# Weight sums of the third product, and the residual's sums of squares, on VectorE instead of GpSimd

## The chip, the cores and the metric

The kernel runs on one core of a Trainium2 chip. The time is device microseconds of one execution, given as the median of several runs.

## The reference

A two-layer decoder trunk over 512 tokens of width 1024. Layer 0 joins native sparse attention with memory cross-attention, layer 1 joins dilated sliding-window attention with memory cross-attention. Each layer ends in the part that the change touches:

```python
def rmsnorm(x, g):
    x32 = x.astype(jnp.float32)
    y = x32 * lax.rsqrt(jnp.mean(x32 * x32, axis=-1, keepdims=True) + EPS)
    return (y * g.astype(jnp.float32)).astype(x.dtype)

def squared_relu_mlp(h, w_up, w_down):
    return jnp.square(jax.nn.relu(h @ w_up)) @ w_down
...
    for layer in range(DEPTH):
        ...
        x = x + squared_relu_mlp(rmsnorm(x, mlp_norm[layer]), w_up[layer], w_down[layer])
```

`w_up` is 1024 x 4096 and `w_down` 4096 x 1024 per layer.

## The kernel before

All of it is float32. A product is made of three matmuls in a packed format (fp32r): each operand is split into a high half, a rounding copy made by ScalarE (line 237 for weights, 282 for activations), and a low half, the rest, made by VectorE (lines 239 and 285). `mm3` multiplies high by high (line 244), then high by low and low by high (line 247).

`mlp` runs a layer's MLP in four quarters of 1024 hidden columns. A quarter has eight steps of the up projection (`n` from 0 to 7, 24 matmuls each: weights through `wload`, Relu and Square on ScalarE at lines 1253 and 1254), and then the down projection as one level of a fast matrix scheme with seven products in place of eight. Each product takes a combination of activation blocks (`combos`, line 1145, makes the combined ones `s12` and `s4`) and a combination of four weight blocks `B[0]` to `B[3]`. The products run in this order, each over two halves `h` of the weights, with 24 matmuls:

| order | code | weights | PSUM | activations |
|---|---|---|---|---|
| P1 | `product(X, blk(0, 0), w11)` | `B[0]` | acc | `s_qk` |
| P2 | `product(Z, blk(0, H), w3)` | `T = B[1] + B[3]` | ps | `s_qk` |
| P3 | `product(Y, s2, w2)` | `T + B[0]` | pt | `s_act` |
| P4 | `product(Z, blk(4, H), w4, True)` | `T + B[0] + B[2]` | ps | `s_qk` |
| P5 | `product(V, s1, w1)` | `U = B[1] + B[0]` | pt | `s_act` |
| P6 | `product(V, s4, w22, True)` | `B[3]` | pt | `s_x` |
| P7 | `product(X, blk(4, 0), ..., True)` | `B[2]` | acc | `s_qk` |

The block sums are running sums in place: `addto` (line 1131) adds a freshly loaded tile to two tiles of 128 x 512, and `wpieces` splits a summed pair into high and low. `w3` splits `T` for P2 and then adds `B[0]` (kept in `b11`) to it, which gives P3's weights; `w2` splits those and then adds `B[2]`, which gives P4's. In each quarter `addto` runs 16 instructions: four that begin `T` during the up projection, four that begin `U`, four in `w3`, four in `w2`. All are on GpSimd. A split weight tile (`s_w`) has four buffers, a loaded one (`s_st`) three, and the activations of a step (`s_p`) six.

The results are scaled per token by `r`, the inverse mean square of the residual, since Relu squared lets the normalisation be applied behind both projections. `inverse` makes `r` in the first quarter of each layer, behind step 0: for each of the eight residual tiles `square` takes the square on ScalarE (line 450) and adds it to one running tile (a copy at line 455, then seven adds at line 457), and four small matmuls (line 482) sum over the partitions. `square` runs the adds on GpSimd unless an engine is given. `r` is first used by `into` (line 1333), behind P2.

The code is written as a plain program; a scheduler in the framework fixes the order of each engine's instructions when the kernel is built, from its own estimate of times, and adds the semaphores. Engines run their own instructions in that order. PE is TensorE, DVE VectorE, ACT ScalarE, POOL GpSimd, SP the queue that issues most loads.

Of the kernel before, what the change touches and what calls it, by code (L numbers as in the profile page):

```python
# [12 lines left out]
ALU = mybir.AluOpType  # L13
# [154 lines left out]
class K:  # L168
# [956 lines left out]
            nc.vector.tensor_tensor(out=self.x[m], in0=ps, in1=xo, op=ALU.add)  # L1125


    def addto(self, out, a, b):

        for i, (o, x) in enumerate(zip(out, a)):  # L1130
            self.nc.gpsimd.tensor_tensor(out=o, in0=x, in1=b[:, i * 512 : (i + 1) * 512], op=ALU.add)  # L1131

    def wpieces(self, t):

# [21 lines left out]
    def mlp(self, l):  # L1156


        nc, ins = self.nc, self.ins
        H = S // 2  # L1160
        x = self.x
# [16 lines left out]
        def inverse():  # L1178

            for k in range(KT):  # L1180
                self.square(k, x[k])
            ps = self.ps(self.pO, [P, NB])
            self.sumsq(ps, self.sq, True, True)
            r, n = [self.c(f"{n}{l}", [P, NB]) for n in ("r2", "n2")]
            nc.vector.tensor_scalar(out=r, in0=ps, scalar1=1.0 / D, scalar2=EPS, op0=ALU.mult, op1=ALU.add)
            nc.vector.reciprocal(out=r, in_=r)
            nc.vector.tensor_scalar(out=n, in0=r, scalar1=-1.0, scalar2=None, op0=ALU.mult)
            return r, n
# [47 lines left out]
        for q in range(4):  # L1236
            a, A12, A4 = [None] * 8, [], []
            B = [ins["w_db"][l, q, i] for i in range(4)]
            U, T = [], []
            for n in range(8):  # L1240
# [25 lines left out]
                if q == 0 and n == 0:  # L1266
                    r, nr = inverse()
# [5 lines left out]
                if n in (5, 6):  # L1273

                    t = [self.t("x", [P, 512]) for _ in range(2)]
# [16 lines left out]
            b11 = []  # L1292
# [11 lines left out]
            def w3(h):  # L1304

                t = T[2 * h : 2 * h + 2]
                w = self.wpieces(t)
                self.addto(t, t, b11[h])
                return w

            def w2(h):
# [31 lines left out]
            for u in range(2):  # L1343
                if q == 0:
                    nc.scalar.activation(G[u], X[u], AF.Copy)
                else:
                    add(G[u], X[u])
            product(Z, blk(0, H), w3)
            into(Z, 1, 1, True)
            Y = two(self.pT)  # L1350
# [463 lines left out]
```

## Time and profile before

| | |
|---|---|
| median of 3 runs | 1276.46 us (1275.83 to 1279.62) |
| profiled execution | 1277.1 us, span 1275.3 us |
| granted TensorE clock, mean | 0.997 |
| TensorE (matmul) busy | 1240.4 us, 97% |
| VectorE busy | 990.8 us, 78% |
| ScalarE busy | 763.3 us, 60% |
| GpSimd busy | 469.4 us, 37% |
| DMA | 139.11 MB, mean 109 GB/s |

Times within the profile are counted from the start of the span. Layer 0's MLP lies between some 325 and 695 us, layer 1's between some 925 us and the end. In a row of the order of time the columns are start, length, engine, line, operation, output<-inputs and shape; in brackets stands the idle time of the engine before it and what ended that. A row of a stretch gives its bounds, its length, then for each engine busy time and number of instructions (PE, weight loads, DVE, ACT, POOL), then the granted clock, the DMA share and GB/s. A row of waits names who waited, for whom, the total in us, the count and the longest.

### The profile page before, as it was taken

To read this page: it belongs to the slowest core of one execution; us is meant where nothing else is said; L and a number is where in the kernel's file an instruction comes from. 1 tells how busy PE (TensorE), PEld (TensorE's weight loads), DVE (VectorE), ACT (ScalarE), POOL (GpSimd) and SP (SyncE) were. 2 spreads that over 40 slices of the span, in tenths; PEclk is the share of its full clock that TensorE was granted. 3 is DMA by queue.
4 is the path that set the end of the run, shared out by engine and by line. 5 is a ranking of instruction groups with operands and counts; after the bars stand their busy time and mean duration, and the time that the engine had idled before them with its cause. 6 is when DMAs were issued, how large, how long until landed. Compare 5 with 4: busy or idle time off the path is not lost.

```text
span 1275.3 us, 18580 instructions
## 1 busy us (share of the span) xinstructions
PE 1240.4 (97%) x6445; PEld 1013.5 (79%) x6445; DVE 990.8 (78%) x1745; ACT 763.3 (60%) x1763; POOL 469.4 (37%) x497
## 2 busy tenths in 40 slices
PE   9998999999999999999999999999999999999998
PEld 8776777677787887888888899888688788888886
DVE  6868878864669678687799968887679868779687
ACT  6666767773466464554656567887776455464462
POOL 0666464533165142260342612222435226034241
PEclk9999999999999999999999999999999999999999
DMA  8312311023432525325235332113241532624423
GB/s 312 112 58 69 100 34 59 10 75 106 151 99 77 175 79 171 125 83 185 97 98 179 104 116 64 62 35 96 69 155 67 178 124 79 187 94 139 141 83 116
DMA packets 52718, 139.11 MB, mean 109 GB/s; under 512 B 5680, under 2 KB 14896, under 8 KB 52624
## 3 DMA queue, kind: packets, MB, share of 16 engines
q1 hardware_dynamic: 51568, 135.50, 33.4%
q0 software_dynamic: 480, 1.38, 0.3%
q8 instruction: 51, 0.84, 0.3%
q10 hardware_dynamic: 576, 1.05, 0.2%
q14 instruction: 43, 0.35, 0.1%
HBM read 132.66 MB, written 5.24 MB: 108 GB/s over the span
## 4 chain that ended last, share of the span: by engine, by line
PE 74%; DVE 17%; ACT 4%; issue 2%; DMA 1%; POOL 1%; SPq 0%; POOLq 0%; DVEq 0%; ACTq 0%
PE s_ps L247 23%; PE s_acc L247 12%; PE s_ps L244 11%; DVE s_w L239 6%; PE s_acc L244 6%; PE s_pt L247 5%; PE s_pt L244 3%; DVE s_p L1145 2%; PE s_po L1080 2%; DVE s_qk L285 1%; PE s_acc L845 1%; ACT s_w L237 1%; PE s_pt L1067 1%; PE s_ps L1031 1%; DVE s_pt L1333 1%
## 5 line engine op out<-in xcount | busy, mean ns | idle before, releaser
L247 PE MATMUL s_ps<-s_act,s_w 128*128 128x512 f32 x1184 | 366.0, 390 | 0.0
L239 DVE TENSOR_TENSOR s_w<-s_st,s_w 128x1024 fp32r<-128x1024 f32 (+4 forms) x161 | 191.1, 1189 | 133.5 <-ACT s_w L237 133.2
L247 PEld LDWEIGHTS s_ps<-s_act,s_w 128*128 128x128 f32 x1184 | 221.8, 188 | 45.7 <-DVE s_act L285 0.4
L237 ACT ACTIVATE s_w<-s_st 128x1024 fp32r<-128x1024 f32 (+4 forms) x182 | 165.7, 918 | 131.0 <-PE s_pt L247 35.6
L244 PE MATMUL s_ps<-s_act,s_w 128*128 128x512 f32 x592 | 231.6, 393 | 3.1 <-DVE s_x L817 1.7
L247 PE MATMUL s_acc<-s_w,s_act 128*128 128x512 f32 (+2 forms) x608 | 169.7, 360 | 2.0 <-DVE s_w L239 1.5
L1131 POOL TENSOR_TENSOR s_x<-s_x,s_st 128x512 f32<-128x512 f32 x64 | 106.0, 1681 | 90.8 <-DVE s_w L239 90.8
L244 PEld LDWEIGHTS s_ps<-s_act,s_w 128*128 128x128 f32 x592 | 110.9, 188 | 28.4 <-ACT s_act L282 3.2
L247 PEld LDWEIGHTS s_acc<-s_w,s_act 128*128 128x128 f32 x608 | 108.9, 190 | 13.1 <-DVE s_w L239 1.6
L244 PE MATMUL s_acc<-s_w,s_act 128*128 128x512 f32 (+2 forms) x304 | 111.0, 370 | 1.9 <-ACT s_w L237 1.9
L1131 POOL TENSOR_TENSOR s_x<-s_qki,s_st 128x512 f32<-128x512 f32 x16 | 26.5, 1654 | 214.9 <-DMA s_st<-in_w_db_dram 195.3
L676 POOL TENSOR_SCALAR s_p<-s_p,s_cr 128x256 f32<-128x256 f32 (+3 forms) x128 | 68.0, 545 | 71.6 <-DVE s_cr L1043 33.4
L239 DVE TENSOR_TENSOR s_w<-s_x,s_w 128x512 fp32r<-128x512 f32 x96 | 88.7, 965 | 5.6 <-ACT s_w L237 5.6
L247 PE MATMUL s_pt<-s_w,s_act 128*128 128x512 f32 x288 | 90.0, 399 | 2.6 <-DVE s_w L239 2.6
L285 DVE TENSOR_TENSOR s_qk<-s_p,s_qk 128x256 fp32r<-128x256 f32 (+1 forms) x96 | 83.9, 886 | 2.8 <-ACT s_qk L282 1.8
L237 ACT ACTIVATE s_w<-s_x 128x512 fp32r<-128x512 f32 x96 | 56.8, 624 | 41.1 <-POOL s_x L1131 41.1
L247 PE MATMUL s_ps<-s_w,s_qk 128*128 128x512 f32 x256 | 78.5, 393 | 2.5 <-DVE s_w L239 2.5
L247 PE MATMUL s_acc<-s_w,s_qk 128*128 128x512 f32 x256 | 76.4, 390 | 0.1
L282 ACT ACTIVATE s_qk<-s_p 128x256 fp32r<-128x256 f32 (+1 forms) x96 | 47.0, 489 | 45.1 <-DVE s_p L1259 42.8
L247 PEld LDWEIGHTS s_pt<-s_w,s_act 128*128 128x128 f32 x288 | 54.0, 191 | 16.9 <-DVE s_w L239 6.0
L1253 ACT ACTIVATE s_p<-s_ps 128x512 f32<-128x512 f32 x64 | 37.8, 591 | 46.8 <-PE s_ps L247 44.4
L244 PEld LDWEIGHTS s_acc<-s_w,s_act 128*128 128x128 f32 x304 | 57.5, 190 | 7.3 <-ACT s_w L237 2.0
(336 smaller groups left out, 2735.8 us busy)
## 6 DMA issues: line engine op xcount, KB each, us to landing
s_st<-in_w_db_dram SPq DMA_DIRECT2D x80, 512.0 KB, 3.6
s_st<-in_w_up_dram SPq DMA_DIRECT2D x64, 512.0 KB, 3.9
s_st<-in_w_bq_dram SPq DMA_DIRECT2D x16, 384.0 KB, 3.1
s_st<-in_w_ag_dram SPq DMA_DIRECT2D x11, 512.0 KB, 4.0
s_act<-in_w_c_dram SPq DMA_DIRECT2D x8, 512.0 KB, 5.8
s_st<-in_w_mem_dram SPq DMA_DIRECT2D x8, 512.0 KB, 3.6
s_st<-in_w_ao_dram SPq DMA_DIRECT2D x16, 256.0 KB, 2.7
s_tq<-in_w_db_dram SPq DMA_DIRECT2D x16, 256.0 KB, 3.2
```

The source lines that it names most:

```text
L237: self.high = nc.scalar.activation(w[:, 0], st, AF.Copy)
L239: self.low = e.tensor_tensor(out=w[:, 1], in0=st, in1=w[:, 0], op=ALU.subtract)
L244: mm(ps, lh[0], rh[0], start=start, stop=False, skip_group_check=again)
L247: self.last = mm(ps, lh[i], rh[j], start=False, stop=stop and i != wr, skip_group_check=again)
L282: nc.scalar.activation(dst[:, 0], src, AF.Copy)
L285: nc.vector.tensor_tensor(out=dst[:, 1], in0=src, in1=dst[:, 0], op=ALU.subtract)
L676: self.nc.gpsimd.tensor_scalar(out=p, in0=p, scalar1=c, scalar2=1.0, op0=ALU.mult, op1=ALU.mult)
L845: nc.tensor.matmul(ps, tbf[:, i].rearrange("p g c -> p (g c)"), ws[j][:, i * 256 : (i + 1) * 256], start=j == 0 and i == 0, stop=j == 3 an ...
L1080: nc.tensor.matmul(O[x * 64 : x * 64 + 64, q0 + o : q0 + 256], v[:, j, br, :], st[x][br][:, j, o:256], start=half == 0 and br == 1 and j = ...
L1131: self.nc.gpsimd.tensor_tensor(out=o, in0=x, in1=b[:, i * 512 : (i + 1) * 512], op=ALU.add)
L1145: tt = lambda o, x, y, op: nc.vector.tensor_tensor(out=o, in0=x, in1=y, op=op)
L1253: nc.scalar.activation(u, ps, AF.Relu)
```

## The change

`addto` takes an engine, and GpSimd stays its default. `w3` gives it VectorE: these four sums of each quarter, 32 in the kernel, move. `inverse` gives `square` VectorE: the copy and the seven adds of each layer, 16 instructions, move. The other twelve sums of a quarter stay on GpSimd.

```diff
-    def addto(self, out, a, b):
+    def addto(self, out, a, b, e=None):
 
         for i, (o, x) in enumerate(zip(out, a)):
-            self.nc.gpsimd.tensor_tensor(out=o, in0=x, in1=b[:, i * 512 : (i + 1) * 512], op=ALU.add)
+            (e or self.nc.gpsimd).tensor_tensor(out=o, in0=x, in1=b[:, i * 512 : (i + 1) * 512], op=ALU.add)
...
         def inverse():
 
             for k in range(KT):
-                self.square(k, x[k])
+                self.square(k, x[k], nc.vector)
...
                 t = T[2 * h : 2 * h + 2]
                 w = self.wpieces(t)
-                self.addto(t, t, b11[h])
+                self.addto(t, t, b11[h], nc.vector)
                 return w
```

For the first residual tile, `square` on VectorE also orders the ScalarE square behind the last weight split issued (lines 451 and 452). The scheduler then arranges the whole order anew. Three places of it follow, as pieces of the difference between the two orders. On VectorE, in quarter 1 of layer 0 from the second split of P2's weights on (`s_w_5338` is P2's second half, `s_w_5361` P3's first, `s_x_...` the tiles of `T`, `s_p_1277` and `s_qk_5262` the last step's activations):

```order
+L1131 TENSOR_TENSOR s_x_5177<-s_x_5177,s_st_5279 128x512
 L239 TENSOR_TENSOR s_w_5338<-s_x_5223,s_w_5338 128x512
+L1131 TENSOR_TENSOR s_x_5178<-s_x_5178,s_st_5279 128x512
 L239 TENSOR_TENSOR s_w_5338<-s_x_5224,s_w_5338 128x512
 L1145 TENSOR_TENSOR s_p_1277_5265<-s_p_1266_5213,s_p_1275_5259 128x256
+L1131 TENSOR_TENSOR s_x_5223<-s_x_5223,s_st_5298 128x512
 L285 TENSOR_TENSOR s_qk_5262<-s_p_1275_5259,s_qk_5262 128x512
+L239 TENSOR_TENSOR s_w_5361<-s_x_5177,s_w_5361 128x512
+L1131 TENSOR_TENSOR s_x_5224<-s_x_5224,s_st_5298 128x512
+L239 TENSOR_TENSOR s_w_5361<-s_x_5178,s_w_5361 128x512
```

The four sums are new here, and the two splits of P3's first half have moved up to them. On VectorE a little later in the same quarter (`s_act_5269` is the low half of the last `s12`, `s_x_5272` of the last `s4`, `s_w_5382` P3's second half, `s_raw` the running result `G`):

```order
-L285 TENSOR_TENSOR s_act_5269<-s_p_1277_5265,s_act_5269 128x512
-L285 TENSOR_TENSOR s_x_5272<-s_p_1268_5219,s_x_5272 128x256
 L1337 TENSOR_TENSOR s_raw_4676<-s_acc_5276,s_raw_4676 128x512
-L239 TENSOR_TENSOR s_w_5361<-s_x_5178,s_w_5361 128x512
 L239 TENSOR_TENSOR s_w_5382<-s_x_5223,s_w_5382 128x512
 L239 TENSOR_TENSOR s_w_5382<-s_x_5224,s_w_5382 128x512
+L1145 TENSOR_TENSOR s_p_1268_5219<-s_p_1275_5259,s_p_1277_5265 128x256
+L285 TENSOR_TENSOR s_act_5269<-s_p_1277_5265,s_act_5269 128x512
```

The low half of the last `s12` has moved from ahead of P3's second half to behind it, and that of `s4` further still. On VectorE at the start of layer 0's MLP (`s_w_4491` and `s_w_4543` are the up projection's weights of steps 5 and 6):

```order
+L455 COPY s_raw_4240<-s_p_1106_4238 128x512
+L457 TENSOR_TENSOR s_raw_4240<-s_raw_4240,s_p_1108_4242 128x512
+L457 TENSOR_TENSOR s_raw_4240<-s_raw_4240,s_p_1109_4245 128x512
 L285 TENSOR_TENSOR s_qk_4231<-s_p_1105_4234,s_qk_4231 128x256
+L457 TENSOR_TENSOR s_raw_4240<-s_raw_4240,s_p_1110_4248 128x512
+L457 TENSOR_TENSOR s_raw_4240<-s_raw_4240,s_p_1111_4251 128x512
 L239 TENSOR_TENSOR s_w_4491<-s_st_4489,s_w_4491 128x1024
-L239 TENSOR_TENSOR s_w_4543<-s_st_4541,s_w_4543 128x1024
```

The squares' copy and adds stand ahead of the split of step 5's weights, and the split of step 6's has moved behind them. The order of the SP queue stays the same but for one weight load of layer 1's attention, which moves ahead of one store.

## The prediction

> **What bounds the kernel now.** I read the page's busy times first, then the stretches by stage, then TensorE's waits, then the order of time around each of them.
>
> ```profile
> PE 1240.4 (97%) x6445; PEld 1013.5 (79%) x6445; DVE 990.8 (78%) x1745; ACT 763.3 (60%) x1763; POOL 469.4 (37%) x497
> 506.00:588.40 82.40, 81.98 (x362) 67.41 (x361) 64.47 (x81) 41.90 (x67) 26.69 (x16) 1.00 0.40 129
> PE s_pt L247 <- DVE s_w L239: 2.6, 4, 1.0
> PE s_ps L247 <- DVE s_w L239: 2.5, 7, 0.4
> ```
>
> TensorE (PE) is busy for 97% of the span, and the third quarter of layer 0's MLP (second row) has 81.98 us of PE in 82.40. So only a wait of PE can be won. In the MLP such waits have nearly one cause: PE stands before the low half of a split weight tile (L239), 5.1 us in 11 places. What they cost is more, because a matmul after a pause starts late; the order of time shows it. I count the seven products of a quarter as they run, P1 to P7, 24 matmuls each: P2 takes w3's weights (the change's "third product"), P3 w2's, P4 w4's. Third quarter, then layer 0's first quarter, then layer 1's:
>
> ```profile
> 567.82 0.39 PE L244 MATMUL s_pt<-s_w,s_act 128*128 128x512 f32 x1
> 573.32 0.39 PE L244 MATMUL s_ps<-s_w,s_qk 128*128 128x512 f32 x1
> 574.81 0.73 PE L247 MATMUL s_ps<-s_w,s_qk 128*128 128x512 f32 x2 [0.42 <-DVE s_w L239]
> 579.50 0.39 PE L244 MATMUL s_pt<-s_w,s_act 128*128 128x512 f32 x1
> 584.94 0.62 PE L244 MATMUL s_acc<-s_w,s_qk 128*128 128x512 f32 x2
> ...
> 400.91 0.39 PE L244 MATMUL s_pt<-s_w,s_act 128*128 128x512 f32 x1
> 404.22 1.20 PE L247 MATMUL s_pt<-s_w,s_act 128*128 128x512 f32 x4 [0.99 <-DVE s_w L239]
> 408.66 0.39 PE L244 MATMUL s_ps<-s_w,s_qk 128*128 128x512 f32 x1
> 414.60 0.39 PE L244 MATMUL s_pt<-s_w,s_act 128*128 128x512 f32 x1
> ...
> 992.06 0.39 PE L244 MATMUL s_pt<-s_w,s_act 128*128 128x512 f32 x1
> 995.41 1.90 PE L247 MATMUL s_pt<-s_w,s_act 128*128 128x512 f32 x4 [0.99 <-DVE s_w L239]
> 1001.45 0.39 PE L244 MATMUL s_ps<-s_w,s_qk 128*128 128x512 f32 x1
> 995.50:999.50 4.00, 4.00 (x11) 3.13 (x12) 4.00 (x5) 1.44 (x3) 4.00 (x3) 0.57 0.31 82
> ```
>
> An undisturbed product takes 584.94 - 579.50 = 5.44 us. In the third quarter P3 takes 5.50 and P4 6.18: 0.80 us lost. The other later quarters have the same single wait (seven of 2.5 us together, one of them layer 0's first quarter), so six later quarters lose about 4.8. Layer 0's first quarter: P3 7.75 and P4 5.94, 2.8 lost. Layer 1's first: P3 9.39, 3.95 lost, since behind the wait the granted clock was 0.57 for 4 us (last row). Together **11.6 us, all that this change can win from these waits**.
>
> **Why the tiles are late.** Third quarter again, VectorE (DVE) and GpSimd (POOL), and last the same place in layer 0's first:
>
> ```profile
> 550.87 0.42 DVE L1145 TENSOR_TENSOR s_p<-s_p,s_p 128x256 f32<-128x256 f32 x1
> 556.00 1.29 DVE L239 TENSOR_TENSOR s_w<-s_x,s_w 128x512 fp32r<-128x512 f32 x2
> 558.29 2.40 DVE L239 TENSOR_TENSOR s_w<-s_x,s_w 128x512 fp32r<-128x512 f32 x2 [1.00 <-ACT s_w L237]
> 560.61 1.50 DVE L1145 TENSOR_TENSOR s_p<-s_p,s_p 128x256 f32<-128x256 f32 x1
> 565.13 0.68 DVE L239 TENSOR_TENSOR s_w<-s_x,s_w 128x512 fp32r<-128x512 f32 x1
> 565.72 0.69 DVE L285 TENSOR_TENSOR s_act<-s_p,s_act 128x512 fp32r<-128x512 f32 x1
> 568.37 2.98 DVE L239 TENSOR_TENSOR s_w<-s_x,s_w 128x512 fp32r<-128x512 f32 x3
> 573.63 2.33 DVE L239 TENSOR_TENSOR s_w<-s_x,s_w 128x512 fp32r<-128x512 f32 x3
> 556.76 6.50 POOL L1131 TENSOR_TENSOR s_x<-s_x,s_st 128x512 f32<-128x512 f32 x4 [7.48 <-DVE s_w L239]
> 565.89 1.67 POOL L1131 TENSOR_TENSOR s_x<-s_x,s_st 128x512 f32<-128x512 f32 x1 [2.62 <-DVE s_w L239]
> 569.12 5.08 POOL L1131 TENSOR_TENSOR s_x<-s_x,s_st 128x512 f32<-128x512 f32 x3 [1.56 <-DVE s_w L239]
> ...
> 392.32 4.69 DVE L239 TENSOR_TENSOR s_w<-s_x,s_w 128x512 fp32r<-128x512 f32 x4
> ```
>
> The same L1145 takes 0.42 us with POOL quiet and 1.50 beside the four POOL sums: each POOL sum holds DVE up for 1.08. These four (556.76 to 563.26) are the sums that the change moves. P3's weights are split from them on DVE at 565.13 and 568.37, POOL's next four sums wait for those splits and end at 574.20, and P4's weights come out of that at 573.63: PE's pause at 574.4.
>
> [...]
>
> **The change, part by part.**
>
> *Weight sums, 32 instructions (4 a quarter).* On DVE each costs a step of 0.59 (565.13 to 565.72), 2.4 us a quarter, and takes 4 x 1.08 = 4.3 us of blocking away. The first piece of DVE's new order, shown with the change, gives the steps; other quarters have the same. The first sum falls into DVE's pause of 1.00 before 558.29; from there nine steps of 0.59 (0.34 for the 256-wide one) put P3's first two splits (s_w_5361) at 562.2 and 563.4 instead of 565.1 and 568.4. POOL's remaining four sums wait for these splits, so they start about 3.6 us sooner, and P4's weights come some 3 us sooner, against a pause of 0.42. The next weight load waits for the buffer that the first two sums read: free at 559.5 by these steps, against 560.0 now (two of four in 6.50). So the later quarters' **4.8 us go**.
>
> Behind the splits now stands the low half of the last combined activation (s_act_5269, the second piece), which P3 needs too. It moved from ahead of three splits to behind them. From 563.4 it has seven steps, 3.6 us, done at 567.0, and with four POOL sums between them (4 x 1.08) at 571.3. PE uses it first in the 23rd matmul of P3: 567.82 + 22 x 0.227 (5.44 / 24) = 572.8. It holds. In the first quarters PE is closer behind: P2's first split runs 8.6 us before P3 (392.32, 400.91), not 11.8 (556.00, 567.82). The same walk from 392.32, 17 steps, gives 401.6 to 405.9, for a need in the 18th matmul, 404.8. That is open, and decides the first quarters.
>
> *Sums of squares, 16 instructions.* POOL's rows, the same work on DVE elsewhere in this kernel, and PE beside it:
>
> ```profile
> 353.15 0.85 POOL L455 COPY s_raw<-s_p 128x512 f32<-128x512 f32 x1 [22.07 <-ACT s_p L450]
> 354.08 11.31 POOL L457 TENSOR_TENSOR s_raw<-s_raw,s_p 128x512 f32<-128x512 f32 x7
> 365.36 1.47 POOL L1131 TENSOR_TENSOR s_x<-s_qki,s_st 128x512 f32<-128x512 f32 x1
> 369.91 1.48 POOL L1131 TENSOR_TENSOR s_x<-s_tq,s_st 128x512 f32<-128x512 f32 x1
> L457 DVE TENSOR_TENSOR s_raw<-s_raw,s_p x7: 684/689/693, 8.7 to 21.5; 128x512 f32<-128x512 f32 x7
> 355.94 1.95 DVE L239 TENSOR_TENSOR s_w<-s_st,s_w 128x1024 fp32r<-128x1024 f32 x1 [0.29 <-ACT s_w L237]
> 364.17 2.94 DVE L1145 TENSOR_TENSOR s_p<-s_p,s_p 128x256 f32<-128x256 f32 x2
> 340.00:356.00 16.00, 16.00 (x81) 13.21 (x81) 8.04 (x12) 11.41 (x19) 2.69 (x3) 1.00 0.43 139
> 356.00:372.00 16.00, 16.00 (x80) 13.46 (x79) 11.58 (x8) 9.10 (x17) 15.00 (x10) 1.00 0.21 66
> ```
>
> At most 8 x 0.69 = 5.5 us of DVE a layer, for 12.2 of POOL. DVE has 8.0 and 4.4 us free in the two stretches and PE does not wait there at all: cost nothing, and PE is covered by weight tiles split ahead. If that cover were gone the price is at most 5.5 us a layer. The adds come ahead of one weight split and let another fall back behind them (third piece), for the tiles of steps 5 and 6, of which the first is split from 355.94 now and needed at about 374 (five times 5.44 us before P3 at 400.9: steps 5 to 7, P1 and P2). What they leave on POOL matters more: the first weight sums, which stood behind the squares until 365.36 to 371.39, start when their load lands, so DVE's pairs such as 364.17 (2.94 for two that take 0.42 alone) run unblocked, and the first quarter's later weights follow. Five blocked rows at 1.08 are 5 us; I take 3 us of lead for the products, near the later quarters' lead. Then the open need above is met (401.6 to 405.9 less 3, against 404.8).
>
> **Sum.** Later quarters -4.8; first quarters -6.75 at best, 0 at worst; I keep 1.5 us for what stays of them: -10.0. The profiled execution took 1277.1 us (span 1275.3), 0.6 over the median 1276.46: 1267.1 in its own terms, 1266.5 against the median. I say **1267**.
>
> **Rivals.**
>
> *The first quarters keep their pause.* The late activation half replaces the late weight tile in P3; for it speaks 405.9 against 404.8, against it the lead from the squares. Gain 4.8 alone: 1272. A pause may also draw the clock down, as layer 1's did and layer 0's did not, 1.6 us more (3.95 - 2.31): 1270 to 1274, inside this rival's chance.
>
> [...]
>
> *No change.* POOL's remaining sums, now sooner, block DVE's splits as before, and the pause moves within the product: 1275 to 1277. Against it: the blocking sums per quarter fall from eight to four.
>
> *Slower.* DVE is the bound in the products: the activation half comes after PE's need in every quarter. By the worst end it is 1.1 us late; with the clock's fall 2.7 a time, 22 in all against 11.6 won: 1287. It decides from 1.45 us a quarter (11.6 / 8); the walk has 1.5 us to spare in six of the eight.
>
> **Chances.** Forecast 0.62 (1264.5 to 1269.5), first quarters keep it 0.20 (1270 to 1274), no change 0.12, slower 0.06. Range 1264 to 1274. A difference under 0.3% (3.8 us) can't be told here from none: faster 0.75, same 0.18, slower 0.07.
>
> **What would show it.** PE's waits for L239 in P3 and P4 gone, later quarters at 81.6 to 81.8 us, no stretch with a granted clock under 0.9 in layer 1's first quarter; POOL near 393 us busy (469 less 24 and 52); DVE busy near 980 in spite of 48 more instructions (+33 us, less 32 x 1.08 and some ten for the squares). Wrong if PE waits in P3 for L285, or if layer B, whose order moves only by a few rows at its start, takes longer.

## The result, and the profile after

Six runs of the changed kernel took 1266.08 us (median; 1264.88 to 1268.47), six of the kernel before beside them 1277.7. The ratio is 0.991, 95% interval 0.9896 to 0.9924: 11.6 us saved. The forecast was 1267 us. The profiled execution took 1264.88 us, its span is 1263.1, which is 12.2 less than before.

The page's busy times after:

```profile
PE 1232.9 (98%) x6445; PEld 1013.6 (80%) x6445; DVE 971.0 (77%) x1793; ACT 762.9 (60%) x1763; POOL 416.2 (33%) x449
```

The row of the third quarter in the view by stretches (from and to, length, then busy time and instructions of PE, its weight loads, DVE, ACT and POOL, then the granted clock), and that of 4 us in P3 of layer 1's first quarter:

```profile
501.33:582.93 81.60, 81.60 (x362) 67.57 (x361) 61.70 (x84) 41.71 (x67) 22.77 (x12) 1.00 0.41 129
986.00:990.00 4.00, 4.00 (x19) 3.32 (x18) 2.56 (x3) 1.84 (x4) 4.00 (x4) 1.00 0.20 57
```

PE is busy for all of the 81.60 us; before, the same quarter had 0.42 us free and was 0.8 longer. VectorE has 61.70 us of work in it against 64.47, though it makes four sums more. In the second place the granted clock, 0.57 before, is 1.00. The order of time on PE, at the heads of P3, P4 and P5, for layer 0's first quarter, its third, and layer 1's first:

```profile
399.90 0.39 PE L244 MATMUL s_pt<-s_w,s_act 128*128 128x512 f32 x1
405.34 0.39 PE L244 MATMUL s_ps<-s_w,s_qk 128*128 128x512 f32 x1
410.78 0.39 PE L244 MATMUL s_pt<-s_w,s_act 128*128 128x512 f32 x1
...
563.10 0.39 PE L244 MATMUL s_pt<-s_w,s_act 128*128 128x512 f32 x1
568.54 0.39 PE L244 MATMUL s_ps<-s_w,s_qk 128*128 128x512 f32 x1
573.98 0.39 PE L244 MATMUL s_pt<-s_w,s_act 128*128 128x512 f32 x1
...
986.84 0.39 PE L244 MATMUL s_pt<-s_w,s_act 128*128 128x512 f32 x1
992.28 0.39 PE L244 MATMUL s_ps<-s_w,s_qk 128*128 128x512 f32 x1
997.72 0.39 PE L244 MATMUL s_pt<-s_w,s_act 128*128 128x512 f32 x1
```

P3 and P4 take 5.44 us each, here and in the other five quarters. PE's waits for L239, 2.6 and 2.5 us in the list of waits before, are not in the list after. Summed over the eight quarters, P3 and P4 had lost 11.92 us against 2 x 5.44 a quarter, and lose nothing now.

The rest of the 12.2 nearly cancels: the last quarter's P7 won 0.4, the opening came out 1.0 us shorter and layer B 1.1 longer, though the order of work is the same in both, but for a few rows at layer B's start. A second profile of the changed kernel (e9, below) bears on these two.

The third quarter on VectorE and GpSimd after (start, duration, and in brackets the idle time before a row and what ended it):

```profile
556.92 0.69 DVE L239 TENSOR_TENSOR s_w<-s_x,s_w 128x512 fp32r<-128x512 f32 x1
557.53 0.68 DVE L1131 TENSOR_TENSOR s_x<-s_x,s_st 128x512 f32<-128x512 f32 x1
558.13 0.69 DVE L239 TENSOR_TENSOR s_w<-s_x,s_w 128x512 fp32r<-128x512 f32 x1
...
561.80 0.68 DVE L285 TENSOR_TENSOR s_act<-s_p,s_act 128x512 fp32r<-128x512 f32 x1
562.40 0.68 DVE L239 TENSOR_TENSOR s_w<-s_x,s_w 128x512 fp32r<-128x512 f32 x1
...
564.94 1.10 DVE L239 TENSOR_TENSOR s_w<-s_x,s_w 128x512 fp32r<-128x512 f32 x1 [1.19 <-ACT s_w L237]
...
557.69 9.50 POOL L1131 TENSOR_TENSOR s_x<-s_x,s_st 128x512 f32<-128x512 f32 x4 [12.98 <-DVE s_w L239]
```

P3's first two splits start at 556.92 and 558.13, P4's first two at 562.40 and 564.94, 3.6 us and more ahead of P4. But the four GpSimd sums that stay take 9.50 us now, where before they took 1.67 and 5.08: here VectorE runs at its full step of 0.60 us and GpSimd is the one that waits.

### The profile page after: what moved, and what is told of

Its sections match the earlier page's. It is cut to its first block, busy times and chain, and to the rows that moved or that the text cites. A ratio compares the mean times of both kernels' runs of the same rounds, so it can differ in the third digit from the quotient of the medians.

```text
span 1263.1 us, 18587 instructions
## 1 busy us (share of the span) xinstructions
PE 1232.9 (98%) x6445; PEld 1013.6 (80%) x6445; DVE 971.0 (77%) x1793; ACT 762.9 (60%) x1763; POOL 416.2 (33%) x449
## 3 DMA queue, kind: packets, MB, share of 16 engines
q10 hardware_dynamic: 576, 1.05, 0.2%
## 4 chain that ended last, share of the span: by engine, by line
PE 87%; DVE 6%; ACT 3%; DMA 2%; issue 1%; POOL 1%; SPq 0%; POOLq 0%; DVEq 0%; ACTq 0%
PE s_ps L247 27%; PE s_ps L244 14%; PE s_acc L247 13%; PE s_pt L247 8%; PE s_acc L244 7%; PE s_pt L244 4%; PE s_po L1080 2%; PE s_acc L845 1%; PE s_ps L1031 1%; PE s_pt L1067 1%; PE s_ps L1541 1%; PE s_pt L701 1%; DVE s_w L263 1%; ACT s_w L237 1%; DMA s_st<-in_w_ag_dram 1%
## 5 line engine op out<-in xcount | busy, mean ns | idle before, releaser
L239 DVE TENSOR_TENSOR s_w<-s_st,s_w 128x1024 fp32r<-128x1024 f32 (+4 forms) x161 | 189.1, 1177 | 133.6 <-ACT s_w L237 133.4
L1131 POOL TENSOR_TENSOR s_x<-s_x,s_st 128x512 f32<-128x512 f32 x32 | 73.9, 2337 | 102.7 <-DVE s_w L239 102.7
L247 PE MATMUL s_pt<-s_w,s_act 128*128 128x512 f32 x288 | 86.7, 390 | 0.0
L239 DVE TENSOR_TENSOR s_w<-s_x,s_w 128x512 fp32r<-128x512 f32 x96 | 68.8, 737 | 10.8 <-ACT s_w L237 10.7
L285 DVE TENSOR_TENSOR s_qk<-s_p,s_qk 128x256 fp32r<-128x256 f32 (+1 forms) x96 | 71.8, 758 | 1.5 <-ACT s_qk L282 0.2
```

The costliest lines, as they stand in the source:

```text
L239: self.low = e.tensor_tensor(out=w[:, 1], in0=st, in1=w[:, 0], op=ALU.subtract)
L247: self.last = mm(ps, lh[i], rh[j], start=False, stop=stop and i != wr, skip_group_check=again)
L285: nc.vector.tensor_tensor(out=dst[:, 1], in0=src, in1=dst[:, 0], op=ALU.subtract)
L1131: (e or self.nc.gpsimd).tensor_tensor(out=o, in0=x, in1=b[:, i * 512 : (i + 1) * 512], op=ALU.add)
```

## The experiments

### One move alone: e1 and e2

```diff
e1:
-                self.square(k, x[k], nc.vector)
+                self.square(k, x[k])
e2:
-                self.addto(t, t, b11[h], nc.vector)
+                self.addto(t, t, b11[h])
```

> Only w3's four sums a quarter move to VectorE; the squares stay on GpSimd. Theory A (the two moves have separate work: the sums clear P4 in every quarter, the squares' leaving gives the first quarter of each layer its lead of some 2.8 us): the later quarters win their 5.5 us, the first quarters keep a pause in P3, because VectorE is no sooner there: layer 0's first quarter still loses 1 to 3 us, layer 1's 1 to 4. Total 1269 to 1273 us. Theory B (the sums alone do everything, the squares are idle baggage): the same time as the full change, 1265 to 1268 us, and no pause of PE in any P3 or P4.

> Only the residual's squares move to VectorE; w3's sums stay on GpSimd. Theory A (separate work): the later quarters keep their pause before P4 as it was (0.8 us each, about 5.5 in all), the first quarters gain from the lead of 2.8 us: their pause in P3 (1.0 us and then 1.0 us and a lower clock) goes or shrinks, P4's stays. A gain of 3 to 6 us: 1271 to 1274 us. Theory B (the squares are idle baggage): within 2 us of the kernel before, 1275 to 1278 us.

Sums alone: 1268.64 us, ratio 0.9935 (0.9919 to 0.9951). Squares alone: 1271.64, ratio 0.9968 (0.9956 to 0.9981). What P3 and P4 lose, from the order of time:

| | layer 0, first quarter | layer 1, first quarter | six later quarters | together |
|---|---|---|---|---|
| before | 2.81 | 3.95 | 5.16 | 11.92 |
| sums alone (e1) | 1.62 | 0.95 | 0.00 | 2.57 |
| squares alone (e2) | 0.03 | 0.75 | 5.37 | 6.15 |
| both (the change) | 0.00 | 0.00 | 0.00 | 0.00 |

Theory B falls for both moves. The later quarters belong to the sums alone. The first quarters are nearly cured by the squares alone, and in good part by the sums alone; each does some of the other's work (9.35 + 5.77 saved apart, 11.92 together). Theory A has the split right, though e1's time lies just under its range; and the pauses stay in other places than A said: e1 keeps its own in P4, not P3, and in e2 P4's in layer 0's first quarter is gone with P3's. In PE's list of waits in e1 (us in total, times, longest) stands a row that neither kernel has:

```profile
PE s_ps L244 <- DVE s_pt L1333: 1.9, 2, 1.3
```

The order of time on VectorE and GpSimd in e1, layer 0's first quarter:

```profile
406.00 1.11 DVE L239 TENSOR_TENSOR s_w<-s_x,s_w 128x512 fp32r<-128x512 f32 x1 [1.84 <-ACT s_w L237]
407.02 0.74 DVE L1333 SCALAR_TENSOR_TENSOR s_pt<-s_ps,n,s_pt 128x512 f32<-128x512 f32 x1
...
408.73 1.51 DVE L285 TENSOR_TENSOR s_x<-s_p,s_x 128x256 fp32r<-128x256 f32 x1
410.16 0.74 DVE L1333 SCALAR_TENSOR_TENSOR s_pt<-s_ps,n,s_pt 128x512 f32<-128x512 f32 x1
...
400.55 9.40 POOL L1131 TENSOR_TENSOR s_x<-s_x,s_st 128x512 f32<-128x512 f32 x4 [12.57 <-DVE s_w L239]
```

P4 adds into the two banks of P2, so it can't touch a bank before `into`'s L1333 row has read it. The split at 406.00 stands in VectorE's order ahead of both, and it waits for a GpSimd sum that came late beside VectorE: VectorE ran without a gap to 404.16, and the four sums took 9.40 us, where one alone takes 1.23 (m1). The second L1333 ends at 410.90; PE, due at the second bank at 409.67, waits 1.28 us for it.

### The same number of sums, elsewhere or not at all: e3 and e4

```diff
e3:
-                self.addto(t, t, b11[h], nc.vector)
+                self.addto(t, t, b11[h])
...
-                self.addto(t, t, self.wdma(B[2][h]))
+                self.addto(t, t, self.wdma(B[2][h]), nc.vector)
e4:
-                self.addto(t, t, b11[h], nc.vector)
```

> The squares on VectorE as in the change, but of the weight sums it is w2's four a quarter that move there, and w3's stay on GpSimd: as many sums moved, one link later in the chain. Theory C (what counts is the chain split, sum, split in front of P4, and any four sums taken out of GpSimd's part of it shorten it): P4's pause goes in the later quarters as with the change, the first quarters may keep part of P3's: 1265 to 1270 us. Theory D (what counts is that nothing of GpSimd stands beside VectorE while it makes P3's weights): no gain in the later quarters, the first ones as with the squares alone: 1271 to 1274 us.

> As the change, but w3's four sums a quarter are left out altogether, on either engine (the third and fourth product of each quarter then take other weights). It bounds what any placing of these sums can win. Theory E (on VectorE the sums cost nothing: their 2.4 us a quarter lie beside PE's work): 1265 to 1268 us, the same as the change. Theory F (their time on VectorE still costs PE something in the first quarters or elsewhere): at least 3 us below the change, 1260 to 1263 us.

e3: 1267.44 us, ratio 0.993 (0.9912 to 0.9947); e4: 1267.24, ratio 0.9931 (0.991 to 0.9951). In both, P3 and P4 take 5.44 us in all eight quarters, as with the change. So C holds: it is the chain of splits and sums in front of P4 that had to be shorter, whichever of the two fours leaves it. And E holds: leaving the sums out wins no more than making them on VectorE. Their 2.4 us a quarter cost PE nothing.

### More on VectorE: e5, e8, and a dose (e6, e7)

e5 gives VectorE the other twelve sums too; e8 gives it w2's beside w3's and leaves the squares on GpSimd. e6 and e7 repeat P2's low halves, once and twice:

```diff
+    def wpieces(self, t, again=0):
...
+            for _ in range(again):
+                self.nc.vector.tensor_tensor(out=p[:, 1], in0=t[i], in1=p[:, 0], op=ALU.subtract)
...
+                w = self.wpieces(t, 1)
```

> All sixteen weight sums of a quarter on VectorE, the squares too: 12 more sums a quarter than the change, 7.2 us, and nothing of GpSimd beside them. Theory G (PE has no wait left in the products, so there is nothing more to win; and VectorE has room, since it is idle for some 18 us of a quarter's 82): 1264 to 1268 us, the same as the change. Theory H (the eight sums added ahead of P1 and the four behind P3's splits make VectorE late for the products): PE waits for VectorE in P3 or P4 again, 1270 us or more.

> As the change, but each of P2's four weight splits is done twice on VectorE (same values): four more VectorE instructions of 0.60 us a quarter, 2.4 us, ahead of all that P3 and P4 need of it. By the trace after the change, what VectorE gives P4 last is room in its banks (the second L1333 row ends at 566.70 in the third quarter, P4 starts at 568.55; in the first it ends at 405.34 with P4 at 405.35). Theory K (a walk along VectorE's order: spare time 1.85 us in a later quarter, none in a first one): 2.4 us lost in each of two first quarters and 0.55 in each of six others, 8 us together: 1272 to 1276. Theory L (VectorE is idle for some 18 us of a quarter and absorbs it): 1264 to 1268.

> As the change, but each of P2's four weight splits is done three times on VectorE: eight more instructions a quarter, 4.8 us. Theory K (spare time 1.85 us in a later quarter, none in a first one): 4.8 us lost in each of two and 2.95 in each of six, 27 us together: 1287 to 1298, slower than before the change. Theory L (absorbed by VectorE's idle time): 1264 to 1268.

> w3's and w2's sums on VectorE, eight a quarter, the squares on GpSimd. With w3's alone the first quarters lost 1.62 and 0.95 us in P4, where VectorE's L1333 stood behind a split that waited for a GpSimd sum of w2, and that sum had lasted longer for VectorE's running without a gap. Theory N (it is that link to GpSimd that costs): without a GpSimd sum between P3's and P4's splits both pauses go, though the squares stay where they were: P3 and P4 at 5.44 us each in all eight quarters, 1265 to 1268 us. Theory O (the first quarters are late for want of the squares' lead of 2.8 us): 1 to 2 us are lost in P3 or P4 of each first quarter, 1268 to 1271 us.

| | us | ratio (95%) | first quarters | a later quarter |
|---|---|---|---|---|
| e5, 16 sums | 1270.41 | 0.9951 (0.9933 to 0.9969) | 81.60 | 82.25 |
| e6, 2.4 us more | 1276.69 | 1.000 (0.9988 to 1.0013) | 81.60, 81.83 | 82.48 |
| e7, 4.8 us more | 1291.08 | 1.0115 (1.0092 to 1.0138) | 83.61, 84.27 | 84.71 |
| e8, 8 sums | 1275.27 | 0.9964 (0.9948 to 0.998) | 81.60 | some 82.5 |

(A quarter's length is from P1's start to the same in the next quarter, for the first quarters in layer 0 and then in layer 1 where they differ; the change has 81.60.) Theory L falls: VectorE's idle time does not absorb work that stands ahead of what PE needs next. Of 2.4 us a quarter PE loses 0.88, of 4.8 it loses 3.11: the first 1.5 to 1.7 us are free, and behind them nearly all counts. K's totals are near (e7's within its range, e6's 0.7 above), but its reason was wrong. It took the second L1333 to be needed at P4's start; in a first quarter PE turns to that bank at P4's seventh matmul, 1.4 us after the start, where e1's pause stands. And e6's first quarters lose 0 and 0.23 us, not 2.4. What PE waits for in its later quarters is a low half of P4's weights (0.39 us, at 490.46 in the second), behind splits that GpSimd holds up again, here in e6's order of time:

```profile
484.94 3.43 DVE L239 TENSOR_TENSOR s_w<-s_x,s_w 128x512 fp32r<-128x512 f32 x2
```

The scheduler arranged all rows anew around the added ones, in layer B too, where e6 lost some 4 us more; so these two are read by their quarters, not their totals. On PE too, P2, P3 and P4 now run into one another; the room that they show is that of their own order, and an estimate for the changed kernel's.

e5 fits neither G nor H: no pause in P3 or P4, but 0.65 us in each later quarter at P7, whose weights ScalarE splits late in the new order. e8 bears N out in the first quarters, where P3 and P4 take 5.44 us with the squares still on GpSimd; yet the time N gave is missed, because VectorE now makes a low half of P7's weights late: by 0.6 us in most later quarters, by 1.9 in the last. PE's waits in e5, of which 1.9 us stand in the opening as before, 0.25 in each later quarter:

```profile
PE s_acc L244 <- ACT s_w L237: 3.4, 7, 1.9
```

In e7, where P3 waits for its weights in every quarter:

```profile
PE s_pt L247 <- DVE s_w L239: 9.8, 15, 0.9
```

And in e8, of which 1.5 us stand in the opening as before:

```profile
PE s_acc L247 <- DVE s_w L239: 6.0, 7, 1.9
```

None of them beats the change.

### The disputed price by itself: m1, m2, m3

The adds were put behind the end of the changed kernel: VectorE and GpSimd adding 128x512 tiles alone, then side by side. The third stretch of m1, in which ScalarE releases both engines, GpSimd three copies later:

```diff
+        start(3)
+        many(nc.vector, d, z, 16)
+        many(nc.gpsimd, p, zz, 4)
```

In m2 VectorE's adds wait for nothing, or each for the one before it. In m3 its rows are weight splits, or sums in place, or both in turn.

> The changed kernel, with five stretches added after its end (so its time is longer by these, and nothing of it is to be compared): 8 adds of 128x512 on VectorE alone; 8 on GpSimd alone; 16 on VectorE, back to back, with 4 on GpSimd released some 2 us after their start; 8 on GpSimd with 12 on VectorE released some 2 us after their start; 12 on VectorE of which one operand comes from PSUM, with 4 on GpSimd. Alone: steps of 0.60 us and 1.3 us. Theory I (as the prediction had it: every GpSimd sum holds VectorE up for 1.08 us): in the third stretch 16 adds take 9.6 + 4 x 1.08 = 13.9 us. Theory J (whichever engine runs without a gap keeps the other out, as the trace after the change suggests): in the third stretch VectorE's 16 adds take 9.6 us as alone and GpSimd's first sum lasts until they end; in the fourth the two alternate, 1.6 us for each pair. In the fifth neither is slowed, by both.

> The changed kernel, again with stretches added after its end (not to be compared in time). In the run before, each VectorE add wrote the tile of the add but one before it and waited for that one's semaphore. Here: 16 adds on VectorE that wait for nothing (each writes another tile) with 4 GpSimd sums released some 2 us after their start; 8 GpSimd sums with 12 such adds released some 2 us after their start; 12 adds of which each takes the result of the one before, with 4 GpSimd sums. Theory M (VectorE keeps GpSimd out as long as its next instruction is ready to go when the one before ends; an instruction that still waits for a semaphore lets GpSimd in): first stretch 9.6 us for the 16 adds and GpSimd's first sum held until they end, 7 us and more; second: the two alternate until the sums are done; third: each GpSimd sum costs VectorE 1.08 us. Theory I (1.08 us for each GpSimd sum whatever VectorE waits for): first stretch 13.9 us, as in the run before.

> The changed kernel with stretches added after its end (not to be compared in time): VectorE runs without a gap, and 4 GpSimd sums are released some 2 us after its start. First 14 weight splits (as L239: a difference of a 128x512 tile and its rounded half), then 14 sums in place (as L1131), then 7 of each in turn, as the changed kernel has them where GpSimd was kept out. Theory P (the kind of VectorE's instruction decides: a sum in place, or a split behind one, keeps GpSimd out): one of the three stretches keeps to steps of 0.60 us, 8.4 us in all, with GpSimd's first sum held for 4 us or more. Theory I (1.08 us for each GpSimd sum, whatever kind): 12.7 us in each stretch.

m1, VectorE and then GpSimd in order of time:

```profile
1283.15 13.98 DVE L1393 TENSOR_TENSOR dve<-src,src 128x512 f32<-128x512 f32 x16 [15.33 <-ACT src L1394]
1301.97 14.11 DVE L1393 TENSOR_TENSOR dve<-src,src 128x512 f32<-128x512 f32 x12 [4.84 <-ACT src L1394]
1316.26 7.33 DVE L1393 TENSOR_TENSOR dve<-s_ps,src 128x512 f32<-128x512 f32 x12 [0.18 <-ACT src L1394]
...
1270.67 9.80 POOL L1393 TENSOR_TENSOR pool<-src,src 128x512 f32<-128x512 f32 x8 [11.48 <-ACT src L1394]
1285.24 6.53 POOL L1393 TENSOR_TENSOR pool<-src,src 128x512 f32<-128x512 f32 x4 [4.77 <-ACT src L1394]
...
1320.33 4.94 POOL L1393 TENSOR_TENSOR pool<-src,src 128x512 f32<-128x512 f32 x4 [7.81 <-ACT src L1394]
```

Theory I holds: 16 x 0.60 + 4 x 1.08 = 13.92, measured 13.98. A hold-up by whole sums, 9.80 / 8 = 1.23 us each alone, would make 9.6 + 4 x 1.23 = 14.5, an estimate from these rows. Theory J falls, though VectorE was first and ran back to back. With one operand from PSUM, VectorE keeps its step (7.33 / 12 = 0.61), and so does GpSimd (4.94 / 4 = 1.24, alone 1.23). m2 and m3 gave the same price in every stretch that mimics the kernel: 13.98 for 16 adds that wait for nothing, 12.77 for 14 splits, 12.78 for 14 sums in place, one GpSimd sum after each VectorE row, four in 6.52 us. Theories M and P fall: neither a wait of VectorE nor the kind of its row explains by itself why GpSimd was kept out in the kernel.

### The change once more: e9

> The changed kernel once more, for a second profile of it. Theory Q (what it won outside the products, 1.0 us in the opening, and what it lost in layer B, 1.1 us with a granted clock of 0.97 between 800 and 860 us, differ from execution to execution): P3 and P4 again 5.44 us in all quarters, but P3 of the first quarter starts anywhere from 399.9 to 402.7 us, and the clock in 800 to 860 us is 1.00 or 0.97. Theory R (they come from the change): P3 of the first quarter at 399.9 us and a clock of 0.97 again, layer B as long as before.

1267.28 us, one run, span 1265.2. P3 and P4 take 5.44 us in all quarters again. Two stretches, e9 first and then the first profile of the changed kernel (the clock is the third number from the end):

```profile
800.00:860.00 60.00, 57.16 (x451) 50.93 (x450) 47.23 (x120) 48.08 (x162) 13.77 (x18) 0.97 0.11 30
100.00:300.00 200.00, 186.82 (x1221) 142.61 (x1220) 151.57 (x407) 140.40 (x431) 106.66 (x158) 0.98 0.19 61
```

```profile
800.00:860.00 60.00, 57.16 (x446) 50.15 (x446) 46.75 (x116) 49.44 (x166) 13.09 (x18) 0.97 0.11 32
100.00:300.00 200.00, 185.97 (x1231) 142.50 (x1230) 151.96 (x409) 140.68 (x431) 105.80 (x158) 1.00 0.20 62
...
828.00:832.00 4.00, 2.77 (x14) 2.19 (x15) 4.00 (x15) 3.54 (x12) 0.00 (x0) 0.83 0.37 98
832.00:836.00 4.00, 4.00 (x28) 4.00 (x28) 2.34 (x9) 3.30 (x12) 0.83 (x1) 0.74 0.24 72
```

The opening differs by 2.3 us between two executions of one program (P3 of the first quarter at 399.90 and at 402.21), with the clock at 1.00 and 0.98. So Q is right there: the 1.0 us of the opening is less than executions of one program differ by, and need not be an effect of the change. Layer B's clock fell in both, to 0.83 and 0.74 in 8 us around 832 in the first, and the kernels m1 to m3, which are the change up to its end, add three executions:

| | clock, 800 to 860 us | layer 0's last matmul of P7 to layer 1's first of P1 |
|---|---|---|
| before, one profile | 1.00 | 301.4 us |
| the change, five profiles | 0.97 in each | 302.3 to 302.6 |
| squares on GpSimd (e1, e8) | 1.00 in both | 300.9 in both |
| squares on VectorE, sums as in e2, e3, e4 | 0.97 in each | 302.6 to 303.0 |

So R is right for layer B, as far as one profile of the kernel before can tell: its 1.1 us come with the change, and in these kernels with the squares on VectorE, not with the sums. The squares alone don't decide it: e5 and e7 have them on VectorE too, and a clock of 1.00 (e6 has 0.97). How they reach layer B is not shown; that they shift where its pauses lie is an argument.

## Why the prediction was right, point by point

- **Only the waits of PE in the products can be won, 11.6 us.** Right: 11.92 measured by the same rule in all eight quarters, all of it won.
- **Later quarters 4.8.** Mis-sized a little: the third quarter (0.80) was taken for all six, and they measure 0.77 to 1.05, 5.16 together, with 0.4 more in the last one's P7.
- **First quarters, "I keep 1.5 us for what stays of them".** This term was the one that was off: nothing stayed. The profiled execution came out 2.2 us below the 1267.1 forecast for it: 1.5 by this term, 0.4 by the later quarters', 0.4 by the last P7, while the opening and layer B cancel, which is luck: the opening differs by 2.3 us from one execution to the next.
- **The walk.** P3's first splits were to start 5.6 and 4.4 us before P3 (562.2 and 563.4 against 567.82); they start 6.2 and 5.0 before it. The two times are where the splits end by the nine steps from 558.29, set beside starts (565.1 and 568.4); by starts the same steps give 561.6 and 562.8, the 6.2 and 5.0 us that came. The low half of `s12` was to be done between 0.8 us before P3's start and 3.5 after; it is done at 562.48, 0.6 before. P4's second split moved from 573.63, 0.3 after P4's start, to 3.6 before it, where "some 3 us" had been said.
- **The open need in the first quarter.** Decided as forecast, but not by the range given: `s_act` was done at 402.48, where 401.6 to 405.9 less 3, less the 1.0 us of the opening, makes 397.6 to 401.9. GpSimd blocked all four rows from 396.27 on, and the high half that the first of them needs came 0.32 us late. The need, 403.75, left 1.3 us.
- **What the walk left out: `into`.** P4 needs the banks that the L1333 rows read, the second of them from its seventh matmul on. In the first quarter that row ended at 405.34, for a need at 405.34 + 6 x 0.227 = 406.70: 1.4 us to spare. e1 shows what it costs when it is late, 1.62 and 0.95 us. The forecast was right with a link missing.
- **Squares cost nothing, and give 3 us of lead.** Right in the MLP, where PE waits for none of it, but not in layer B, whose 1.1 us come with them (e9). The lead is right: P2's first split runs 11.4 us before P3 instead of 8.6 (388.49 to 399.90), the same in e2 (11.5), and 8.0 in e1. The reason was right as well: the first of GpSimd's weight sums starts at 353.73 instead of 365.36. But the second waits for PE until 361.90, so the four end 4.5 us sooner, not 11. GpSimd's first two of these sums after, in the order of time:

```profile
353.73 1.28 POOL L1131 TENSOR_TENSOR s_x<-s_qki,s_st 128x512 f32<-128x512 f32 x1 [23.66 <-DVE s_raw L457]
361.90 1.30 POOL L1131 TENSOR_TENSOR s_x<-s_tq,s_st 128x512 f32<-128x512 f32 x1 [6.89 <-PE s_pt L1175]
```

- **1.08 us for each GpSimd sum.** Right as a price (m1: 13.92 by it, 13.98 measured); a sum itself takes 1.23 us alone (m1), where the rows before show 1.62 to 1.67 beside VectorE (6.50 / 4; 565.89). It was wrong as a rule for the remaining sums: in the later quarters they hardly held VectorE up and were held up instead (9.50 us for the four of the third quarter, against 1.67 and 5.08). That is why POOL is busy for 416.2 us and not 393 (32 sums at 2.34 us on average, 1.68 before: 21 us), and VectorE for 971.0 and not 980.
- **The rival "slower", which "decides from 1.45 us a quarter; the walk has 1.5 us to spare".** The size is borne out by the dose, if not the place: 1.5 to 1.7 us are free in a later quarter, and with 4.8 more the kernel is slower than before.
- **The signs.** PE's waits for L239 in P3 and P4 are gone, the later quarters take 81.60 us and PE waits for no L285 in P3, as said. But one sign of being wrong came: layer B takes 1.1 us longer. The forecast had no term for it. It is small against the 11.9 us won and goes with the squares (e9); why is open.
- **The rivals "first quarters keep their pause" and "no change".** Neither came. The first is what e1 does, with L1333 in place of the late activation half.

## What to carry to other kernels

When two engines pass tiles back and forth in front of a third, count the links of that chain before the next need, and move work so that a link goes, not so that an engine's busy share falls: four sums a quarter and the squares won 11.9 us here, twelve sums more won nothing. Walk the whole order of the engine that receives the work up to every row that the bound engine waits for, buffers to be freed included, and note which row stands behind another's wait. Measure the room with a dose of repeated work: of some 20 us of VectorE's idle time in a quarter, some 1.5 could be used ahead of P3 and P4.

## What the runs showed of the hardware that was not expected

Two engines that block each other need not share the loss alike. In the eight stretches beside each other (m1 to m3) GpSimd got in after each VectorE row: four sums took 6.26 to 6.53 us and eight 12.49 to 12.50, at a price of 1.08 us each to VectorE (m1, 13.98 us in all). In the changed kernel it was kept out through up to six rows, until VectorE paused or took an operand from PSUM: its first two sums in the third quarter took 2.61 and 3.98 us (557.69, 560.26), one in layer 1's first quarter 4.75 (981.99). They ended 1.23 us behind the start of a row with an operand from PSUM (559.07, 563.01) and 1.15 behind the start of a pause (985.59).

The traces show what goes with it. In all eight quarters of the changed kernel GpSimd's first sum starts 0.16 us after the start of one of VectorE's sums (557.69 against 557.53) and doesn't get in at the next row, which takes 0.69 us (558.13); e1's first quarter has the same start (400.55 against 400.39), and so has e6's second (481.04 against 480.88). In all eight of the kernel before it starts 0.16 us after the start of a split (393.08 against 392.92), and gets in at the next row, which takes 1.79 us there (393.52), or in a pause ahead of it. In m1 to m3 GpSimd got in beside sums too, but where it came second there it came 0.28 us or more after the start of a row (1301.56 against 1301.28 in m3). So the kind of row together with the moment is a rival that no run tried, and what decides it was not found; waits, kinds of rows and their order were tried (m2, m3).

The granted clock can fall behind like pauses in one kernel and not in another. PE's pauses in layer B before, in the order of time:

```profile
834.46 0.38 PE L247 MATMUL s_acc<-s_w,s_act 128*128 128x256 f32 x1 [0.54 <-DVE s_w L263]
835.70 0.37 PE L1493 MATMUL s_pt<-idr,s_ki 128*128 128x128 f32 x2 [0.58 <-ACT s_qk L659]
836.90 0.36 PE L1493 MATMUL s_pt<-idr,s_ki 128*128 128x128 f32 x2 [0.46 <-DVE s_tq L1462]
```

The clock there before, by stretches (after: the two rows of 4 us around 832, above):

```profile
834.00:838.00 4.00, 2.51 (x16) 1.98 (x17) 4.00 (x14) 3.68 (x13) 0.13 (x1) 1.00 0.34 100
```

The same pauses after, in the order of time:

```profile
828.16 0.38 PE L247 MATMUL s_acc<-s_w,s_act 128*128 128x256 f32 x1 [0.51 <-DVE s_w L263]
829.43 0.36 PE L1493 MATMUL s_pt<-idr,s_ki 128*128 128x128 f32 x2 [0.61 <-ACT s_qk L659]
830.63 0.50 PE L1493 MATMUL s_pt<-idr,s_ki 128*128 128x128 f32 x2 [0.46 <-DVE s_tq L1462]
```

Three like pauses in both; behind the third the granted clock falls after (0.83, then 0.74) and not before (1.00), and the same two transposes take 0.50 us for 0.36. No pause in these rows is longer than 0.61 us. The fall came in all five profiles of the change (0.97 from 800 to 860 us, the table of e9) and neither in the one of the kernel before nor in that of e1 (1.00 in both), whose pauses are like these (0.51, 0.61 and 0.46 us in e1). What decides it stays open.
